# Strassen's algorithm for the gate and up products of two FFNs, and a down product in three chunks

## The chip, the cores and the metric

The kernel runs on one core of a Trainium2 chip. The metric is the device time of one execution in microseconds (us): 1136.71 us is the median of three runs before the change (1136.51 to 1138.03). The core has TensorE (PE) for matrix products, VectorE (DVE), ScalarE (ACT) and GpSimd (POOL) for elementwise work, and SyncE (SP), which issues the DMAs here. Each engine works through its own queue in order and waits on semaphores for the others. Products land in PSUM, and are read from there by VectorE and ScalarE.

## What is computed

The reference is one decoder layer over 512 tokens of width 1024, all in float32. Two of its sub-layers are the same gated FFN, one at the start and one at the end, with a hidden width of 2816; between them lie a token mixer and a cross-attention, which the change leaves alone.

```python
def rmsnorm(t, g):
    tf = t.astype(F32)
    y = tf * lax.rsqrt(jnp.mean(tf * tf, axis=-1, keepdims=True) + NORM_EPS)
    return (y * g.astype(F32)).astype(t.dtype)

def swiglu(h, w_gate, w_up, w_down):
    return (jax.nn.silu(h @ w_gate) * (h @ w_up)) @ w_down

h = rmsnorm(x, ffn1_norm[l])
x = x + 0.5 * swiglu(h, ffn1_w_gate[l], ffn1_w_up[l], ffn1_w_down[l])
...
h = rmsnorm(x, ffn2_norm[l])
x = x + 0.5 * swiglu(h, ffn2_w_gate[l], ffn2_w_up[l], ffn2_w_down[l])
return rmsnorm(x, final_norm)
```

## The kernel before

Activations are held transposed: X is eight tiles (`KD` = 8) of 128 channels by 512 tokens. Weights come tile by tile, so that one tile of a gate or up matrix is 128 outputs by 1024 inputs, as eight blocks of 128 x 128. The hidden width has 22 such tiles (`NF`), numbered f.

*Products in three parts.* To keep float32 precision, every operand is split in two (`split`, L102 to L105): ScalarE copies it to a rounded high part (L103), VectorE subtracts that to get the low part (L104). A product is then three matmuls (`mm3`, L124 to L129): high by high, high by low, low by high, accumulated in one PSUM bank. `load_weight` (L109) takes one of three raw buffers (tag `wraw`), loads it by a DMA on SP's queue, and splits it to one of three pairs `whi` and `wlo`.

*The norm is applied late.* `Norm.split` (L199) writes the high and low parts hH and hL of x times its gain; the factor of each token, R, is worked out beside the first matmuls (`factor`, L233: sums of squares that GpSimd adds up at L170, a column of them by TensorE, the inverse root by VectorE, and a broadcast by TensorE) and multiplied in when a product is read out of PSUM.

*The FFN* (`ffn`, L214). Two chunks of 11 hidden tiles (`NCHUNK`, `CF`). For each tile f the gate and the up product are run, each 8 x 3 matmuls of 512 columns into a bank of its own; `evacuate` (L241) multiplies both by R, applies SiLU, multiplies them and splits the result to hidH and hidL. After a chunk comes its part of the down product: for each of the eight output tiles d, 11 x 3 matmuls (`down_tile`, L219), after which VectorE adds half of it to X[d] (L230). In the second chunk of the first FFN, each finished X[d] goes to the next norm at once (`nxt.add`). In the last chunk of the last FFN the down product is run over the first and then the second half of the tokens, in matmuls of 256 columns, so that the final norm and the output of one half lie beside the products of the other; six of its eight weight tiles are kept for the second half (`weights`, L295), and the first two output tiles begin without the last hidden tile.

*Buffers and order.* PSUM has eight banks, four under `acc` and four under `aux`. The pool `hp` has 40 slots of 128 x 512 for split activations and a few others. The order of each engine's queue is made by a scheduler when the kernel is built: it goes by the order of the program where it can, and puts an instruction ahead of earlier ones that are not ready. GpSimd is used for sums of squares, a mask and a few memsets, and does nothing during gate, up and the first chunk of down, but for the memory rows.

Of the kernel before, what the change touches and what calls it, by code (L numbers as in the profile page):

```python
# [17 lines left out]
F32 = mybir.dt.float32  # L18
F32R = mybir.dt.float32r
# [5 lines left out]
P = 128  # L25
S = 512
# [1 line left out]
KD = D // P  # L28
FF = 2816
NF = FF // P  # L30
NCHUNK = 2
CF = NF // NCHUNK
NM = 256
NT = S // P
ATT_SCALE = 0.125
# [19 lines left out]
def body(tc, I, out):  # L55
# [3 lines left out]
    with ctx:  # L59
# [151 lines left out]
                self.square(d)  # L211


        def ffn(norm, gate, up, down, nxt, first=None, between=None):  # L214
            h = (norm.H, norm.L)
            with tc.tile_pool(name="ffn", bufs=2) as fp:
                R = None

                def down_tile(d, w, hid, tok, jj, acc=None, js=range(CF)):  # L219

                    if acc is None:
                        acc = acc_tile()[:, tok]
                    for (wH, wL), (j0, j1) in zip(w, jj):
                        for j in range(j0, j1):
                            if j in js:
                                mm3(acc, (wH, wL), hid, (slice(None), j - j0),
                                    (j, slice(None), tok), j == 0, j == CF - 1)
                    if CF - 1 not in js:
                        return acc
                    nc.vector.scalar_tensor_tensor(X[d][:, tok], acc, 0.5, X[d][:, tok],  # L230
                                                   op0=ALU.mult, op1=ALU.add)
# [6 lines left out]
                                norm.square(d)  # L238
                    return rows(norm.stats.column(D))

                def evacuate(ps, hid):  # L241
                    gp = fp.tile([P, S], F32, name="gp", tag="gp")
                    nc.vector.tensor_mul(gp, ps[0], R)  # L243
                    s = fp.tile([P, S], F32, name="s", tag="s")
                    nc.scalar.activation(s, gp, AF.Silu)
                    u = fp.tile([P, S], F32, name="u", tag="u")
                    nc.vector.tensor_mul(u, ps[1], R)  # L247
                    nc.vector.tensor_mul(u, s, u)
                    hH = fp.tile([P, S], F32R, name="hidH", tag="hidH", bufs=12)
                    hL = fp.tile([P, S], F32R, name="hidL", tag="hidL", bufs=12)  # L250
                    split(hH, hL, u)
                    hid[0].append(hH)
                    hid[1].append(hL)

                pending = []
                halves = ((0, 6), (6, CF))
                for c in range(NCHUNK):
                    hid = ([], [])
                    for j in range(CF):
                        f = c * CF + j  # L260
                        ps = []
                        for src in (gate, up):
                            if f == 0 and src is gate and first is not None:
                                w = first()
                            else:
                                w = load_weight(src[f], [KD, P])
                            acc = acc_tile()
                            for k in range(KD):
                                mm3(acc, w, h, (slice(None), k), k, k == 0, k == KD - 1)
                            ps.append(acc)  # L270
                            if first is not None and f == 1 and R is None:
                                R = factor()
                        pending.append(ps)
                        if first is not None and f == 0:
                            continue
                        if R is None:
                            R = factor()
                        while pending:
                            evacuate(pending.pop(0), hid)
                    if c < NCHUNK - 1 or nxt is not None:  # L280
                        for d in range(KD):
                            w = [load_weight(down[c, d, :, j0:j1, :], [j1 - j0, P])
                                 for j0, j1 in halves]
                            down_tile(d, w, hid, slice(0, S), halves)
                            if c == NCHUNK - 1:
                                nxt.add(d)
                            elif between is not None:
                                between(d)
                        continue


                    thirds = ((0, 4), (4, 8), (8, CF))
                    kept = {}

                    def weights(d, keep):  # L295
                        if d in kept:
                            return kept[d], thirds
                        if not keep:
                            return [load_weight(down[c, d, :, j0:j1, :], [j1 - j0, P])
                                    for j0, j1 in halves], halves  # L300
                        kept[d] = []
                        for j0, j1 in thirds:
                            raw = wp.tile([P, j1 - j0, P], F32, name="wraw3", tag="wraw")
                            nc.sync.dma_start(raw, down[c, d, :, j0:j1, :])
                            pair = tuple(h_tile("wk")[:, :(j1 - j0) * P]
                                         .rearrange("p (j m) -> p j m", m=P) for _ in range(2))
                            split(*pair, raw)
                            kept[d].append(pair)
                        return kept[d], thirds

                    for t0 in range(0, S, S // 2):
                        tok = slice(t0, t0 + S // 2)
                        stats = Stats(KD, S // 2, 1)
                        early = {}
                        if t0 == 0:
                            for d in range(2):
                                w, cut = weights(d, True)
                                early[d] = down_tile(d, w, hid, tok, cut, None, range(CF - 1))
                        for d in range(KD):
                            w, cut = weights(d, d < 6)  # L320
                            if d in early:
                                down_tile(d, w, hid, tok, cut, early[d], range(CF - 1, CF))
                            else:
                                down_tile(d, w, hid, tok, cut)
                            stats.add(X[d][:, tok])
                        R = rows(stats.column(D), 2, None)
                        for d in range(0, KD, 2):
                            o = fp.tile([P, 2, S // 2], F32, name="o", tag="o", bufs=4)
                            for e in range(2):
                                nc.vector.scalar_tensor_tensor(  # L330
                                    o[:, e], X[d + e][:, tok], gcol(G_FIN, d + e), R,
                                    op0=ALU.mult, op1=ALU.mult)
                            nc.sync.dma_start(out[d:d + 2, :, tok].rearrange("d p t -> p d t"), o)
# [495 lines left out]

def _down(w):  # L830

    return np.ascontiguousarray(w.reshape(NCHUNK, CF, P, KD, P).transpose(0, 3, 2, 1, 4))


def pack(x, mem, positions, ffn1_norm, ffn1_w_gate, ffn1_w_up, ffn1_w_down,
# [48 lines left out]
```

## Time and profile before

| | |
|---|---|
| median of 3 runs | 1136.71 us (1136.51 to 1138.03) |
| the profiled execution | 1139.12 us |
| its span, first to last instruction | 1137.3 us |
| mean granted TensorE clock | 0.993 of full speed |
| instructions | 13932, of which 5472 matmuls |
| moved by DMA | 110.79 MB, 97 GB/s over the span |

In the profile, L12 is line 12 of the kernel; PE and PEld are TensorE's matmuls and its weight loads, which overlap; a window or a row of the order of time starts with microseconds from the start of the span. A row of a group gives line, engine, operation, output and inputs, shapes and count, then busy time and mean length, then the idle time before it and what ended that. A row of the order of time gives its start, its length, engine, line, operation, tiles, and in brackets how long the engine had been idle and what released it. Matmuls are pipelined, so the length of one is more than the distance to the next, and the distance of starts says how fast they go.

### The profile page before, as it was taken

The numbers are of one execution on the slowest core, as the hardware profiler recorded it, in microseconds if no ns is written. First come the engines' busy times: TensorE is split into PE (matmuls) and PEld (weight loads), VectorE is DVE, ScalarE is ACT, GpSimd is POOL, SyncE is SP. The second block draws the span as 40 slices with busy tenths as digits, with TensorE's granted clock in tenths as the row PEclk, the third lists the DMA queues.
The fourth block names the chain that finished last, engine by engine and source line by source line (L and its number), as shares of the span: only waits on it lengthen the run. The fifth ranks groups of instructions, "written<-read, shape, count | busy, mean of one in ns | idle before, by whom it ended". The sixth has DMA issues, their size and how long they took to land. (4 is left out here: it accounts for less than half of the span.)

```text
span 1137.3 us, 13932 instructions
## 1 busy us (share of the span) xinstructions
PE 1121.1 (99%) x5472; PEld 936.4 (82%) x5472; DVE 589.2 (52%) x1023; ACT 422.6 (37%) x668; POOL 66.2 (6%) x82
## 2 busy tenths in 40 slices
PE   9999999999999999999999999999999999999996
PEld 7788888888888888877868988778888888888996
DVE  4544533444344456578797555455444334445542
ACT  6332322332233433567655344433222222233420
POOL 2000100000002000001121000120000000000011
PEclk9999999999999999999989999999999999999998
DMA  6322333222233423010135412132232333323511
GB/s 218 112 93 88 114 97 128 93 93 94 83 88 114 141 93 108 25 45 29 41 111 196 165 63 74 47 102 93 95 99 75 89 125 97 108 93 113 154 63 38
DMA packets 39698, 110.79 MB, mean 97 GB/s; under 512 B 4432, under 2 KB 9296, under 8 KB 39632
## 3 DMA queue, kind: packets, MB, share of 16 engines
q1 hardware_dynamic: 39632, 109.89, 30.1%
q8 instruction: 43, 0.70, 0.2%
q14 instruction: 23, 0.19, 0.1%
HBM read 107.78 MB, written 2.10 MB: 97 GB/s over the span
## 5 line engine op out<-in xcount | busy, mean ns | idle before, releaser
L103 ACT ACTIVATE whi<-wraw 128x1024 fp32r<-128x1024 f32 (+2 forms) x213 | 202.8, 953 | 522.0 <-PE acc L128 300.9
L104 DVE TENSOR_TENSOR wlo<-wraw,whi 128x1024 fp32r<-128x1024 f32 (+2 forms) x213 | 238.4, 1120 | 166.7 <-ACT whi L103 166.4
L127 PE MATMUL acc<-hH,whi 128*128 128x512 f32 x768 | 300.8, 392 | 0.6 <-ACT hH L202 0.6
L128 PE MATMUL acc<-hL,whi 128*128 128x512 f32 x768 | 299.3, 390 | 0.8 <-DVE hL L203 0.8
L129 PE MATMUL acc<-hH,wlo 128*128 128x512 f32 x768 | 299.3, 390 | 0.5 <-DVE wlo L104 0.5
L128 PEld LDWEIGHTS acc<-hL,whi 128*128 128x128 f32 x768 | 144.3, 188 | 31.6 <-DVE hL L203 1.5
L127 PEld LDWEIGHTS acc<-hH,whi 128*128 128x128 f32 x768 | 144.3, 188 | 31.6 <-ACT hH L202 1.0
L129 PEld LDWEIGHTS acc<-hH,wlo 128*128 128x128 f32 x768 | 144.2, 188 | 30.6 <-DVE wlo L104 1.0
L127 PE MATMUL acc<-hidH,whi 128*128 128x512 f32 (+1 forms) x308 | 115.5, 375 | 0.0
L129 PE MATMUL acc<-hidH,wlo 128*128 128x512 f32 (+1 forms) x308 | 115.3, 374 | 0.0
L128 PE MATMUL acc<-hidL,whi 128*128 128x512 f32 (+1 forms) x308 | 115.3, 374 | 0.0
L170 POOL TENSOR_TENSOR sq<-sq 128x512 f32<-128x512 f32 (+1 forms) x39 | 49.3, 1265 | 778.8 <-ACT sq L178 778.4
L247 DVE TENSOR_TENSOR u<-acc,R 128x512 f32<-128x512 f32 x44 | 30.4, 690 | 121.6 <-PE acc L129 121.6
L243 DVE TENSOR_TENSOR gp<-acc,R 128x512 f32<-128x512 f32 x44 | 30.4, 691 | 85.6 <-PE acc L129 81.7
L128 PEld LDWEIGHTS acc<-hidL,whi 128*128 128x128 f32 x308 | 58.0, 188 | 10.3
L127 PEld LDWEIGHTS acc<-hidH,whi 128*128 128x128 f32 x308 | 58.0, 188 | 10.2
L129 PEld LDWEIGHTS acc<-hidH,wlo 128*128 128x128 f32 x308 | 58.0, 188 | 10.2
L127 PE MATMUL acc<-whi,hH 128*128 128x512 f32 x160 | 62.6, 391 | 0.0
L129 PE MATMUL acc<-whi,hL 128*128 128x512 f32 x160 | 62.4, 390 | 0.0
L128 PE MATMUL acc<-wlo,hH 128*128 128x512 f32 x160 | 62.3, 389 | 0.0
L230 DVE SCALAR_TENSOR_TENSOR x<-acc,x 128x512 f32<-128x512 f32 (+1 forms) x40 | 23.3, 584 | 75.0 <-PE acc L129 75.0
L178 ACT ACTIVATE sq<-x 128x512 f32<-128x512 f32 (+1 forms) x48 | 26.0, 551 | 41.8 <-DVE x L230 39.2
(211 smaller groups left out, 1476.6 us busy)
## 6 DMA issues: line engine op xcount, KB each, us to landing
wraw<-up SPq DMA_DIRECT2D x44, 512.0 KB, 3.5
wraw<-gate SPq DMA_DIRECT2D x43, 512.0 KB, 3.4
wraw<-down SPq DMA_DIRECT2D x28, 384.0 KB, 3.1
wraw<-w_in SPq DMA_DIRECT2D x20, 512.0 KB, 3.5
wraw<-down SPq DMA_DIRECT2D x28, 320.0 KB, 2.8
wraw<-w_out SPq DMA_DIRECT2D x16, 256.0 KB, 2.6
wraw<-wv SPq DMA_DIRECT2D x8, 512.0 KB, 3.4
wraw<-wk SPq DMA_DIRECT2D x8, 512.0 KB, 4.0
```

The lines of the kernel that those rows point to most:

```text
L103: ins = nc.scalar.activation(hi, src, AF.Copy)
L104: nc.vector.tensor_sub(lo, src, f32(hi))
L127: nc.tensor.matmul(ps, lhsT=aH, rhs=bH, start=start, stop=False)
L128: nc.tensor.matmul(ps, lhsT=aH, rhs=bL, start=False, stop=False)
L129: nc.tensor.matmul(ps, lhsT=aL, rhs=bH, start=False, stop=stop)
L170: nc.gpsimd.tensor_add(self.parts[0], self.parts[0], sq)
L178: nc.scalar.activation(sq, src, AF.Square)
L230: nc.vector.scalar_tensor_tensor(X[d][:, tok], acc, 0.5, X[d][:, tok], op0=ALU.mult, op1=ALU.add)
L243: nc.vector.tensor_mul(gp, ps[0], R)
L247: nc.vector.tensor_mul(u, ps[1], R)
```

## The change

The gate and up products of the hidden tiles 2 to 21 are computed by a form of Strassen's algorithm with seven products instead of eight. The three halvings are: two weight tiles a1 and a2 (outputs), blocks 0 to 3 against 4 to 7 of the input channels, and tokens 0 to 255 (`LO`) against 256 to 511 (`HI`). Each of the seven products has 4 x 3 matmuls of 256 columns.

- `sums_of_h`, once for each FFN after hidden tile 0, builds sums and differences of the quarters of x times gain, and splits them (T13 and T24, 16 tiles of `hp`).
- `strassen_weights` loads two raw weight tiles, forms the sums of their halves (two on GpSimd, two on VectorE) and splits the seven left operands.
- `strassen` runs the products in the order 1, 2, 6, 5, 7, 3, 4. Products 1, 6, 7 and 4 accumulate in one `acc` bank, z; product 2 has an `aux` bank, 5 and 3 share another. ScalarE copies z after products 1 and 6, and the bank of product 5, to SBUF; VectorE adds up the four output quarters and multiplies them by R.
- Hidden tiles 0 and 1 stay plain products (`plain`, `evacuate`).
- The down product follows in three chunks of 8, 8 and 6 hidden tiles. In each, two output tiles start without the last pair of hidden tiles (three in the last chunk of the last FFN, where all eight weight tiles are now kept). The rotary tables and memory rows (`between`) move from the first chunk of the first FFN to its last.
- The FFN's pool is laid out anew, with working tiles shared under the tags `c` and `half`; the high parts of the hidden tiles move to `hp`.

```diff
-NCHUNK = 2
-CF = NF // NCHUNK
...
+        LO, HI = slice(0, S // 2), slice(S // 2, S)
+        KH = KD // 2
+        def sums_of_h(norm):
+            T13, T24 = ([], []), ([], [])
+            for k in range(KH):
+                xg = []
+                for d in (k, k + KH):
+                    t = hp.tile([P, S], F32, name="xg", tag="h")
+                    nc.vector.tensor_scalar_mul(t, X[d], gcol(norm.off, d))
+                    xg.append(t)
+                a, b = xg
+                t13 = hp.tile([P, S], F32, name="t13", tag="h")
+                nc.vector.tensor_sub(t13[:, LO], a[:, HI], a[:, LO])
+                nc.vector.tensor_sub(t13[:, HI], b[:, HI], a[:, HI])
+                t24 = hp.tile([P, S], F32, name="t24", tag="h")
+                nc.vector.tensor_sub(t24[:, LO], b[:, HI], t13[:, LO])
+                nc.vector.tensor_sub(t24[:, HI], b[:, LO], t24[:, LO])
+                for t, pair in ((t13, T13), (t24, T24)):
+                    pair[0].append(h_tile("tH"))
+                    pair[1].append(h_tile("tL"))
+                    split(pair[0][k], pair[1][k], t)
+            return T13, T24
...
-            with tc.tile_pool(name="ffn", bufs=2) as fp:
+            with tc.tile_pool(name="ffn", bufs=1) as fp:
...
+                def hidden(u, hid):
+                    hH, hL = h_tile("hidH"), fp.tile([P, S], F32R, name="hidL", tag="hidL", bufs=8)
+                def evacuate(ps, hid):
+                    gp = c_tile("gp")
+                    nc.vector.tensor_mul(gp, ps[0], R)
+                    nc.scalar.activation(gp, gp, AF.Silu)
+                    u = c_tile("u")
+                    nc.vector.tensor_mul(u, ps[1], R)
+                    nc.vector.tensor_mul(u, gp, u)
+                    hidden(u, hid)
...
+                def strassen_weights(src, j):
+                    a1 = wp.tile([P, KD, P], F32, name="wraw", tag="wraw")
+                    a2 = wp.tile([P, KD, P], F32, name="wraw2", tag="wraw")
+                    last["dma"] = nc.sync.dma_start(a1, src[2 * j])
+                    last["dma"] = nc.sync.dma_start(a2, src[2 * j + 1])
+                    k0, k1 = slice(0, KH), slice(KH, KD)
+                    s13 = fp.tile([P, 2, KH, P], F32, name="s13", tag="s13", bufs=2)
+                    nc.gpsimd.tensor_add(s13[:, 0], a2[:, k0], a2[:, k1])
+                    nc.gpsimd.tensor_sub(s13[:, 1], a1[:, k0], a2[:, k0])
+                    w1 = (wp.tile([P, KD, P], F32R, name="whi", tag="whi"),
+                          wp.tile([P, KD, P], F32R, name="wlo", tag="wlo"))
+                    split(w1[0], w1[1], a1)
+                    nc.vector.tensor_sub(a2[:, k0], s13[:, 0], a1[:, k0])
+                    w24 = tuple(fp.tile([P, 2, KH, P], F32R, name="w24" + n, tag="w24" + n, bufs=2)
+                                for n in "hl")
+                    split(w24[0][:, 0], w24[1][:, 0], a2[:, k0])
+                    w13 = tuple(fp.tile([P, 2, KH, P], F32R, name="w13" + n, tag="w13" + n)
+                                for n in "hl")
+                    split(w13[0], w13[1], s13)
+                    nc.vector.tensor_sub(a1[:, k0], a1[:, k1], a2[:, k0])
+                    split(w24[0][:, 1], w24[1][:, 1], a1[:, k0])
+                    w22 = tuple(fp.tile([P, KH, P], F32R, name="w22" + n, tag="w22" + n, bufs=2)
+                                for n in "hl")
+                    split(w22[0], w22[1], a2[:, k1])
+                    def of(w, i):
+                        return tuple(x[:, i] for x in w)
+                    return {1: of(w1, k0), 2: of(w1, k1), 6: of(w24, 0), 5: of(w13, 0),
+                            7: of(w13, 1), 3: of(w24, 1), 4: w22}
+                def strassen(src, j, T):
+                    w = strassen_weights(src, j)
+                    T13, T24 = T
+                    right = {1: (h, 0, LO), 2: (h, KH, LO), 3: (h, KH, HI), 4: (T24, 0, HI),
+                             5: (T13, 0, LO), 6: (T24, 0, LO), 7: (T13, 0, HI)}
+                    def product(ps, i, start):
+                        b, k0, tok = right[i]
+                        wH, wL = w[i]
+                        for k in range(KH):
+                            bH, bL = b[0][k0 + k][:, tok], b[1][k0 + k][:, tok]
+                            for n, (x, y) in enumerate(((wH, bH), (wH, bL), (wL, bH))):
+                                nc.tensor.matmul(ps, lhsT=x[:, k], rhs=y,
+                                                 start=start and k == 0 and n == 0,
+                                                 stop=k == KH - 1 and n == 2,
+                                                 skip_group_check=True)
+                    z = acc_tile()[:, HI]
+                    product(z, 1, True)
+                    p1 = half_tile("p1")
+                    nc.scalar.activation(p1, z, AF.Copy)
+                    b1 = aux_tile()[:, HI]
+                    product(b1, 2, True)
+                    c1, c2 = c_tile("c1"), c_tile("c2")
+                    nc.vector.tensor_add(c1[:, LO], b1, p1)
+                    product(z, 6, False)
+                    v = half_tile("v")
+                    nc.scalar.activation(v, z, AF.Copy)
+                    b5 = aux_tile()[:, HI]
+                    product(b5, 5, True)
+                    p5 = half_tile("p5")
+                    nc.scalar.activation(p5, b5, AF.Copy)
+                    product(z, 7, False)
+                    nc.vector.tensor_add(c2[:, HI], z, p5)
+                    product(b5, 3, False)
+                    nc.vector.tensor_add(c1[:, HI], b5, v)
+                    product(z, 4, False)
+                    nc.vector.tensor_mul(c2[:, LO], z, R[:, LO])
+                    nc.vector.tensor_mul(c1, c1, R)
+                    nc.vector.tensor_mul(c2[:, HI], c2[:, HI], R[:, HI])
+                    return c1, c2
+                T = None
+                chunks = ((0, 4), (4, 8), (8, NF // 2))
+                for c, (j0, j1) in enumerate(chunks):
+                    for j in range(j0, j1):
+                        if j == 0:
+                            pending = []
+                            for f in (0, 1):
+                                ps = [plain(f, gate)]
+                                if f == 1 and R is None:
+                                    R = factor()
+                                ps.append(plain(f, up))
+                                pending.append(ps)
+                                if first is None and f == 0:
+                                    R = factor()
+                                if R is not None:
+                                    while pending:
+                                        evacuate(pending.pop(0), hid)
+                                if f == 0:
+                                    T = sums_of_h(norm)
+                            continue
+                        g = strassen(gate, j, T)
+                        for t in g:
+                            nc.scalar.activation(t, t, AF.Silu)
+                        u = strassen(up, j, T)
+                        for a, b in zip(g, u):
+                            nc.vector.tensor_mul(b, a, b)
+                            hidden(b, hid)
+                    f0, n = 2 * j0, 2 * (j1 - j0)
+                    if c < len(chunks) - 1 or nxt is not None:
+                        early = {}
+                        for d in range(2):
+                            w = [load_weight(down[d, :, f0:f0 + n, :], [n, P])]
+                            early[d] = w, down_tile(d, w, hid, slice(0, S), None, range(n - 2))
+                        for d in range(KD):
+                            if d in early:
+                                w, acc = early[d]
+                                down_tile(d, w, hid, slice(0, S), acc, range(n - 2, n))
...
+                    cut = ((0, 4), (4, 6))
...
+                            for d in range(3):
+                                early[d] = down_tile(d, weights(d), hid, tok, None, range(n - 2),
+                                                     cut)
...
-    return np.ascontiguousarray(w.reshape(NCHUNK, CF, P, KD, P).transpose(0, 3, 2, 1, 4))
+    return np.ascontiguousarray(w.reshape(NF, P, KD, P).transpose(2, 1, 0, 3))
```

108 lines of the change are left out of this document (38 added, 70 removed).

## The prediction

> **What bounds the kernel now.** I read the page first: busy shares, then the chain that ended last; after that the windows of the stages, the order of time, and the groups by line and shape.
>
> ```profile
> PE 1121.1 (99%) x5472; PEld 936.4 (82%) x5472; DVE 589.2 (52%) x1023; ACT 422.6 (37%) x668; POOL 66.2 (6%) x82
> ...
> PE 32%; DVE 0%; issue 0%; ACT 0%; DVEq 0%; ACTq 0%
> 131.00:219.00 88.00, 88.00 (x392) 72.92 (x391) 35.60 (x53) 21.77 (x27) 0.00 (x0) 1.00 0.32 100
> 13.30:34.30 21.00, 20.47 (x95) 15.87 (x93) 10.16 (x22) 10.04 (x15) 7.77 (x6) 1.00 0.49 162
> 763.80:782.80 19.00, 18.98 (x84) 15.20 (x85) 9.36 (x23) 6.85 (x8) 0.00 (x0) 1.00 0.32 103
> ```
>
> TensorE is busy nearly all the span, the chain of waits names hardly anything else, and in the first down product (131 to 219 us) VectorE works 35.6 of 88 us and ScalarE 21.8 (columns of a window: its length, then PE, PEld, DVE, ACT, POOL busy). The granted clock is 1.00. So the kernel is bound by how many matmuls TensorE streams, and busy time misleads there, since neighbours overlap. The pitch has to come from starts:
>
> ```profile
> 1029.66 0.39 PE L127 MATMUL acc<-hH,whi 128*128 128x512 f32 x1
> ...
> 1046.89 0.39 PE L128 MATMUL acc<-hL,whi 128*128 128x512 f32 x1
> ...
> 1060.26 0.28 PE L127 MATMUL acc<-hidH,wk 128*128 128x256 f32 x1
> ...
> 1076.93 0.28 PE L128 MATMUL acc<-hidL,wk 128*128 128x256 f32 x1
> ```
>
> Between the first two lie 76 steps, 17.23/76 = 0.2267 us for 512 columns; between the last two 139 steps, 16.67/139 = 0.120 us for 256 columns. Half the columns cost 53%, not 50%. The profiled execution took 1139.12 us (span 1137.3), the median is 1136.71. I add differences to the median.
>
> **The change, part by part.**
>
> *Matmuls of gate and up.* Two output tiles of one weight matrix now take 2 x 8 x 3 = 48 matmuls of 512 columns, 48 x 0.2267 = 10.88 us. A Strassen call has 7 products of 4 x 3 matmuls of 256 columns, 84 x 0.120 = 10.08 us. That is 0.80 us less, not the eighth that 7 for 8 suggests. Tiles 0 and 1 stay plain, so there are 10 pairs x 2 matrices x 2 FFNs = 40 calls: **-32.0 us** of matmul.
>
> *Down in chunks of 8, 8 and 6.* The number of matmuls is the same. In the last FFN the half-token part shrinks from 11 tiles to 6: 2 x 8 x 5 x 3 = 240 matmuls of 0.120 become 120 of 0.2267, 28.8 against 27.2: **-1.6 us**. Eight more residual updates per FFN (L230, about 0.69 us each) lie beside down products in which VectorE is 60% idle. A third handover from hidden tiles to down is added per FFN; two d tiles started early without the last pair give 2 x 6 x 3 x 0.2267 = 8.2 us of cover, against about 5 us to finish a pair (working below). I cost it at nothing; without that cover it would be 5 us each, 10 in all. The rotary tables and memory rows move to the last chunk: a few us of ACT and DVE under 4 us of PE per tile, nothing.
>
> *What a call costs the other engines.*
>
> ```profile
> L104 DVE TENSOR_TENSOR wlo<-wraw,whi 128x1024 fp32r<-128x1024 f32 x139 | 173.2, 1246 | 100.9 <-ACT whi L103 100.7
> L103 ACT ACTIVATE whi<-wraw 128x1024 fp32r<-128x1024 f32 x139 | 147.2, 1060 | 376.9 <-PE acc L128 184.9 <-issue 150.2 <-PE acc L129 40.3
> L103 ACT ACTIVATE hidH<-u 128x512 fp32r<-128x512 f32 x44 | 27.8, 633 | 35.2 <-DVE u L248 35.2
> L103 ACT ACTIVATE kH<-acc 128x256 fp32r<-128x256 f32 x8 | 2.9, 365 | 0.0
> L230 DVE SCALAR_TENSOR_TENSOR x<-acc,x 128x256 f32<-128x256 f32 x16 | 6.7, 424 | 30.1 <-PE acc L129 30.1
> L509 DVE TENSOR_SCALAR s<-s,rz 128x512 f32<-128x512 f32 x8 | 3.9, 481 | 0.0
> 34.24 0.68 DVE L247 TENSOR_TENSOR u<-acc,R 128x512 f32<-128x512 f32 x1
> 34.84 0.68 DVE L243 TENSOR_TENSOR gp<-acc,R 128x512 f32<-128x512 f32 x1
> 699.20 1.23 DVE L104 TENSOR_TENSOR wlo<-wraw,whi 128x1024 fp32r<-128x1024 f32 x1 [3.23 <-ACT whi L103]
> 700.34 0.68 DVE L104 TENSOR_TENSOR qL<-acc,qH 128x512 fp32r<-128x512 f32 x1
> ```
>
> Back to back, VectorE takes 0.60 us for 512 elements and 1.14 for 1024, so about 0.33 for 256. Per call: weights 2 x 1.14 + 5 x 0.60 = 5.3; collecting the products 5 x 0.33 + 0.60 = 2.3; the hidden tiles of a pair (two products, two low parts, 2.4) shared by two calls 1.2. Together **8.8 us of VectorE per 10.08 us of PE**. ScalarE: 2 x 1.06 + 3 x 0.63 + 3 x 0.37 + 1.25 = 6.4 us. GpSimd, idle here until now, gets two sums of 512 per call, and these are not free for VectorE:
>
> ```profile
> 737.04 0.75 DVE L203 SCALAR_TENSOR_TENSOR hL<-x,gains,hH 128x512 fp32r<-128x512 f32 x1
> ...
> 738.30 1.72 DVE L104 TENSOR_TENSOR wlo<-wraw,whi 128x1024 fp32r<-128x1024 f32 x1
> 739.95 1.77 DVE L203 SCALAR_TENSOR_TENSOR hL<-x,gains,hH 128x512 fp32r<-128x512 f32 x1
> 737.14 1.80 POOL L170 TENSOR_TENSOR sq<-sq 128x512 f32<-128x512 f32 x1 [2.88 <-ACT sq L178]
> 739.81 1.36 POOL L170 TENSOR_TENSOR sq<-sq 128x512 f32<-128x512 f32 x1 [0.87 <-ACT sq L178]
> 584.83 0.68 DVE L619 TENSOR_TENSOR yo<-acc,R 128x512 f32<-128x512 f32 x1
> 584.62 1.41 POOL L170 TENSOR_TENSOR sq<-sq 128x512 f32<-128x512 f32 x1 [0.27 <-ACT sq L178]
> ```
>
> Beside a GpSimd sum the same low part took 1.77 instead of 0.75 us, and a weight's 1.72 instead of 1.23: 1.0 and 0.5 lost, a mean of 0.75. The op at 584.83, which reads PSUM and one SBUF tile, lost nothing. The Trainium skill, "SBUF — State Buffer", section "Who interferes with whom", says that a VectorE instruction with two SBUF inputs and a GpSimd instruction that reads SBUF exclude each other, the later one blocking fully. These rows agree, and by that rule a sum could cost VectorE its whole length; it is rival A that carries this.
>
> Two sums at 0 to 1.36 us each cost VectorE 0 to 2.7 us per call; I take 1.5, from the two rows, so 10.3 us per call. That exceeds 10.08, but calls aren't all alike. Before chunks 1 and 2 stands a down product of 8 x 24 x 0.2267 = 43.5 us with about 8 x (1.14 + 0.60) = 14 us of VectorE in it, so the weights of the first call and a half, about 10 us, can be ready. Chunk 1 then needs 8 x 10.3 - 10 = 72 of 80.6 us. Chunk 0 (6 calls) has no such lead: 62 for 60.5 us. What stays is jitter: z, one PSUM bank, passes 1, 6, 7, 4, and PE may go on only when it has been read. Each handover is covered by one product, 12 x 0.120 = 1.44 us. The read of z after product 7 is VectorE's (0.42 us); behind a blocked op of 1.72 that has just begun, PE waits 0.7 us. Such ops fill about a third of a call, so about 0.15 us on the mean; ScalarE's three reads (0.37 behind at most 1.06) just fit. With chunk 0's deficit and misplaced queue orders I take 0.3 us per call, bounds 0 and 1.4 (VectorE at 8.8 + 2.7): **+12 us** (0 to 57). DMA bytes of gate and up are unchanged; down has fewer transfers.
>
> *The sums of h.* At each FFN's start VectorE gets 8 scalings (481 ns, 0.40 back to back), 16 halves at 0.33 and 8 low parts at 0.60: 13.3 us; ScalarE 8 x 0.63 = 5. They run beside tiles 0 and 1.
>
> ```profile
> 16.33 8.17 POOL L170 TENSOR_TENSOR sq<-sq 128x512 f32<-128x512 f32 x6 [15.89 <-ACT sq L178]
> 34.38 0.51 PE L127 MATMUL acc<-hH,whi 128*128 128x512 f32 x1
> 763.81 0.50 PE L128 MATMUL acc<-hL,whi 128*128 128x512 f32 x1 [0.48 <-DVE hL L203]
> 778.60 1.22 DVE L104 TENSOR_TENSOR wlo<-wraw,whi 128x1024 fp32r<-128x1024 f32 x1
> ```
>
> FFN2: from the last hL (763.8) to the end of tile 1 (about 782.8) VectorE works 9.4 us, 1.2 of it for a tile 2 that is gone, so 10.8 are free. Needed before product 6, which first reads the sums, are 13.3 + w1 1.14 + w24 1.2 + lock 1.5 = 17.1, less 2.9 for products 1 and 2: about 4 us late. FFN1: from 13.3 to 34.3 us VectorE works 10.2 us, 2.5 for tile 2, so 13.3 are free; needed are 17.1 + 6 x 0.75 for the squares that GpSimd adds there, less 2.9: about 6 us late. **+10 us**, bounds 4 (gaps used better) and 25 (all behind PE).
>
> *Sum:* -32.0 - 1.6 + 10 + 12 = -11.6, so 1136.7 - 11.6 = **1125 us**.
>
> **The rivals.**
>
> A, *VectorE becomes the bound through the GpSimd sums* (slower). For it: 8.8 us of work, of which only five small ops read PSUM, and the 1.0 us in the 739.95 row. Against: idle VectorE in down. An in-order VectorE that is late with z holds PE, so the lead is worth less than I count. At 11.0 us per call (8.8 + 2 x 1.1) the 12 become 37: 1150 us. It decides from 10.67 us per call, (33.6 - 10)/40 = 0.59 over the matmuls.
>
> B, *three raw buffers feed two raw tiles per call* (slower). The next a2 can only load when a1 is done with.
>
> ```profile
> wraw<-up SPq DMA_DIRECT2D x44, 512.0 KB, 3.5
> ```
>
> Then 3.5 for the DMA, 2 x 1.36 to 1.8 for the sums, and about 4.3 for the differences and their parts follow: 10.5 to 11.4 us a call. Against: two buffers of each derived tile and the lead absorb most within 8 calls. At 10.9 the 12 become 33: 1146 us.
>
> C, *all is hidden*: starts cost 4, calls 0.1 each: 1136.7 - 33.6 + 8 = 1111 us.
>
> D, *a draw*: stalls eat the 33.6 us nearly exactly, 1134 to 1139.
>
> **How the numbers follow.** Forecast 0.36, C 0.17, D 0.12, A 0.23, B 0.12. Faster by over 0.2% (what a measurement can tell from no change): 0.53; within it 0.12; slower 0.35. The range reaches from C's better half, 1107, to A with 11.2 us per call, 1160; about 2 in 10 lie outside. Where the time is shorter, 1112 to 1134 is the forecast's own range.
>
> **What would show it.** Matmuls of 256 columns at 0.120 us in the calls, calls of 10.2 to 10.6 us; DVE near 90% in Strassen stretches; low parts of 1.7 us beside POOL; PE idle at product 6 of each FFN's first call, 4 to 6 us in sum. A call length over 10.7 us with PE released by DVE would prove A, with ACT or POOL waiting for wraw B. A pitch over 0.126 would undo the first term.

## The result, and the profile after

The changed kernel takes 1207.22 us (median of 4 runs, 1204.36 to 1210.1) against 1136.97 us before: 1.062 times the time, 95% interval 1.058 to 1.065. It was forecast at 1125 us, with a range from 1107 to 1160. The profiled execution has a span of 1208.1 us, 70.8 more than before.

The page of the changed kernel, busy times and the chain that ended last:

```profile
PE 1121.5 (93%) x6792; PEld 991.7 (82%) x6792; DVE 805.9 (67%) x1445; ACT 529.2 (44%) x906; POOL 182.9 (15%) x162
...
PE 45%; DVE 12%; POOL 4%; DMA 4%; ACT 2%; issue 2%; DVEq 0%; POOLq 0%; ACTq 0%; SPq 0%
```

Before, the chain held little but TensorE. Now VectorE, GpSimd and DMAs stand in it with a fifth of the span: something makes TensorE wait. The windows of the first FFN's three Strassen stretches (6, 8 and 6 calls):

```profile
47.80:118.70 70.90, 65.58 (x507) 62.94 (x506) 55.66 (x89) 34.40 (x60) 13.62 (x10) 0.96 0.31 98
162.10:257.30 95.20, 84.53 (x674) 82.69 (x673) 68.93 (x112) 43.31 (x74) 16.47 (x13) 0.98 0.30 95
300.70:372.10 71.40, 63.86 (x506) 62.58 (x505) 51.71 (x93) 32.12 (x57) 10.86 (x9) 0.98 0.31 100
```

A call takes 70.9/6, 95.2/8 and 71.4/6 = 11.8 to 11.9 us, where its matmuls need 10.08; yet VectorE, the third figure after the length, is busy 72 to 79%, not 90%. So a bound of plain VectorE work isn't what one sees. Counted from the first start of a stretch to the start that follows its last matmul, these are 70.8, 95.1 and 71.2 us, and those of the second FFN 76.9, 94.6 and 72.4. Added up by such starts, the difference to before is:

| stretch | forecast, us | measured, us |
|---|---|---|
| fewer and shorter matmuls | -33.6 | -33.6 |
| 40 calls over 10.08 us each (480.8 - 403.2) | +12 | +77.6 |
| first call of FFN1 at 47.8, tile 2 before at 34.4 | +6 | +13.4 |
| second FFN, first matmul to first call, 26.3 against 24.6 | +4 | +1.7 |
| last down product of FFN1, 39.5 against 144 x 0.2267 = 32.6 | 0 | +6.9 |
| end of the last call to the end of the span, 54.1; before 77.1, less 240 x 0.120 | 0 | +5.8 |

That makes 71.8 us. The other -1.0 is lost by the kernel before: its first down product (132.5 to 193.3 us) takes 60.8 us, where 264 matmuls need 59.8.

Inside a call, one can see it happen. The order of time of the changed kernel, first TensorE, then ScalarE, VectorE and GpSimd at the same place:

```profile
212.34 0.28 PE L345 MATMUL aux<-hH,wlo 128*128 128x256 f32 x1
...
212.69 0.28 PE L345 MATMUL aux<-hH,wlo 128*128 128x256 f32 x1
...
213.06 0.28 PE L345 MATMUL aux<-hH,wlo 128*128 128x256 f32 x1
214.82 0.38 PE L345 MATMUL acc<-tH,w24h 128*128 128x256 f32 x1 [1.49 <-ACT p L353]
...
217.67 0.28 PE L345 MATMUL aux<-tH,w13l 128*128 128x256 f32 x1
218.88 0.39 PE L345 MATMUL acc<-tH,w13h 128*128 128x256 f32 x1 [0.94 <-ACT v L360]
```
```profile
212.40 0.63 ACT L101 ACTIVATE w24h<-wraw 128x512 fp32r<-128x512 f32 x1 [3.77 <-DVE wraw L313]
212.94 1.04 ACT L101 ACTIVATE whi<-wraw 128x1024 fp32r<-128x1024 f32 x1
213.89 0.61 ACT L101 ACTIVATE w22h<-wraw 128x512 fp32r<-128x512 f32 x1
214.41 0.36 ACT L353 ACTIVATE p<-acc 128x256 f32<-128x256 f32 x1
```
```profile
207.69 0.42 DVE L366 TENSOR_TENSOR c<-acc,p 128x256 f32<-128x256 f32 x1 [0.39 <-PE acc L345]
211.62 0.69 DVE L313 TENSOR_TENSOR wraw<-s,wraw 128x512 f32<-128x512 f32 x1 [3.52 <-POOL s L308]
```
```profile
209.05 1.28 POOL L307 TENSOR_TENSOR s<-wraw 128x512 f32<-128x512 f32 x1 [6.36 <-DMA wraw<-up]
210.30 1.29 POOL L308 TENSOR_TENSOR s<-wraw,wraw 128x512 f32<-128x512 f32 x1
```

Read from below: GpSimd gets a2 at 209.05 and has both sums at 211.6. VectorE has stood 3.5 us with the difference (L313) at the head of its queue. ScalarE has stood 3.8 us behind it, and then splits three weights of a later call before it copies z (214.41). TensorE waits for that copy 1.5 us, and at 218.88 for the next one. All its waits for these two copies add up to 34.9 us. All 40 differences together kept VectorE idle 95.3 us:

```profile
L308 POOL TENSOR_TENSOR s<-wraw,wraw 128x512 f32<-128x512 f32 x40 | 60.0, 1499 | 0.0
L307 POOL TENSOR_TENSOR s<-wraw 128x512 f32<-128x512 f32 x40 | 56.6, 1415 | 536.3 <-DMA wraw<-gate 292.6 <-DMA wraw<-up 182.5 <-DVE c L368 26.8
...
L313 DVE TENSOR_TENSOR wraw<-s,wraw 128x512 f32<-128x512 f32 x40 | 27.7, 691 | 95.3 <-POOL s L308 95.3
L102 DVE TENSOR_TENSOR w24l<-wraw,w24h 128x512 fp32r<-128x512 f32 x80 | 54.3, 684 | 4.1 <-ACT w24h L101 3.7
```

(groups by line and shape of the changed kernel). The last row matters too: the low parts w24l keep their 684 ns, so the sums do not lengthen them here. The first reading was therefore rival B: a2 comes late because three raw buffers feed two tiles a call. GpSimd's 475.1 us of waiting for wraw (second row) is also the sign that the prediction had named for B.

Part of the loss is a slower clock. In eleven pieces of 3.4 to 10.2 us, 58 us together, the granted clock is half, and matmuls of 256 columns then start 0.213 us apart instead of 0.120. The kernel before has one such piece of 6.8 us (both have one more at the end of the span, not counted here). One of the eleven, as a window and in the order of time:

```profile
172.30:175.40 3.10, 3.10 (x16) 3.10 (x16) 2.13 (x4) 0.95 (x1) 0.00 (x0) 0.50 0.00 0
```
```profile
172.66 0.41 PE L345 MATMUL acc<-tL,w13h 128*128 128x256 f32 x1
...
175.22 0.41 PE L345 MATMUL aux<-hL,w24h 128*128 128x256 f32 x1
```

Summed over the matmuls in these pieces that is about 17 us against 3 before, some 10 of them in the calls. This is worked out from the starts; no run here tests it apart from the waits.

### The profile page after: what moved, and what is told of

It reads as the page before. It is cut to its first block, busy times and chain, and to the rows that moved or that the text cites. A ratio compares the mean times of both kernels' runs of the same rounds, so it can differ in the third digit from the quotient of the medians.

```text
span 1208.1 us, 17314 instructions
## 1 busy us (share of the span) xinstructions
PE 1121.5 (93%) x6792; PEld 991.7 (82%) x6792; DVE 805.9 (67%) x1445; ACT 529.2 (44%) x906; POOL 182.9 (15%) x162
## 4 chain that ended last, share of the span: by engine, by line
PE 45%; DVE 12%; POOL 4%; DMA 4%; ACT 2%; issue 2%; DVEq 0%; POOLq 0%; ACTq 0%; SPq 0%
PE acc L127 10%; PE acc L125 10%; PE acc L126 10%; PE acc L345 5%; PE aux L345 3%; DMA wraw<-up 2%; PE aux L125 2%; POOL s L308 2%; POOL s L307 2%; PE aux L127 2%; PE aux L126 2%; DMA wraw<-gate 2%; DVE wlo L102 1%; DVE w13l L102 1%; DVE w24l L102 1%
## 5 line engine op out<-in xcount | busy, mean ns | idle before, releaser
L102 DVE TENSOR_TENSOR wlo<-wraw,whi 128x1024 fp32r<-128x1024 f32 (+2 forms) x157 | 187.2, 1194 | 86.6 <-ACT whi L101 86.4
L307 POOL TENSOR_TENSOR s<-wraw 128x512 f32<-128x512 f32 x40 | 56.6, 1415 | 536.3 <-DMA wraw<-gate 292.6
L125 PE MATMUL acc<-hidH,whi 128*128 128x512 f32 x304 | 119.3, 392 | 0.0
L127 PE MATMUL acc<-hidH,wlo 128*128 128x512 f32 x304 | 119.0, 392 | 0.0
L126 PE MATMUL acc<-hidL,whi 128*128 128x512 f32 x304 | 118.9, 391 | 0.0
L313 DVE TENSOR_TENSOR wraw<-s,wraw 128x512 f32<-128x512 f32 x40 | 27.7, 691 | 95.3 <-POOL s L308 95.3
L101 ACT ACTIVATE w24h<-wraw 128x512 fp32r<-128x512 f32 x80 | 49.6, 626 | 76.3 <-DVE wraw L313 44.5
L126 PEld LDWEIGHTS acc<-hidL,whi 128*128 128x128 f32 x304 | 57.5, 189 | 11.8
L125 PEld LDWEIGHTS acc<-hidH,whi 128*128 128x128 f32 x304 | 57.5, 189 | 11.8
L345 PE MATMUL acc<-tH,w13h 128*128 128x256 f32 x160 | 48.6, 304 | 19.5 <-ACT v L360 19.5
L308 POOL TENSOR_TENSOR s<-wraw,wraw 128x512 f32<-128x512 f32 x40 | 60.0, 1499 | 0.0
L102 DVE TENSOR_TENSOR w24l<-wraw,w24h 128x512 fp32r<-128x512 f32 x80 | 54.3, 684 | 4.1 <-ACT w24h L101 3.7
L127 PE MATMUL acc<-hH,wlo 128*128 128x512 f32 x128 | 50.9, 398 | 3.8 <-DVE wlo L102 3.8
```

What stands on the lines that cost most here:

```text
L101: ins = nc.scalar.activation(hi, src, AF.Copy)
L102: nc.vector.tensor_sub(lo, src, f32(hi))
L125: nc.tensor.matmul(ps, lhsT=aH, rhs=bH, start=start, stop=False)
L126: nc.tensor.matmul(ps, lhsT=aH, rhs=bL, start=False, stop=False)
L127: nc.tensor.matmul(ps, lhsT=aL, rhs=bH, start=False, stop=stop)
L307: nc.gpsimd.tensor_add(s13[:, 0], a2[:, k0], a2[:, k1])
```

## The experiments

Each time here, but for the versions at the end, is the median of two executions, which lie up to 4 us apart.

**A fourth raw buffer.** If B holds, this frees the way.

```diff
-                    return fp.tile([P, S], F32, name=name, tag="c", bufs=5)
+                    return fp.tile([P, S], F32, name=name, tag="c", bufs=4)
...
-                    return fp.tile([P, S // 2], F32, name=name, tag="half", bufs=5)
+                    return fp.tile([P, S // 2], F32, name=name, tag="half", bufs=3)
...
-                    a2 = wp.tile([P, KD, P], F32, name="wraw2", tag="wraw")
+                    odd.append(j)
+                    pool, tag = (wp, "wraw") if len(odd) % 2 else (fp, "raw4")
+                    a2 = pool.tile([P, KD, P], F32, name="wraw2", tag=tag)
```

> A fourth raw buffer in the FFN's pool (every second a2), paid for with the small buffers (p1, v, p5: 3 instead of 5; c: 4 instead of 5). Theory B (the way of a2 from the release of a1's buffer through DMA, GpSimd sums and VectorE differences sets the length of a call, and ScalarE and VectorE stand in their queues behind it while PE waits for the copies of z): a call falls from 11.85 to 10.3 to 10.8 us, 40 x 1.0 to 1.5 = 40 to 60 us less, 1147 to 1167 us; GpSimd's wait for the DMA of a2 is no longer what VectorE waits on. Theory A (VectorE with the lock of the GpSimd sums is the bound): nothing changes, 1200 to 1210 us.

**Its control**, the smaller buffers alone (the first two edits, and the tag `c` of the last tile `o` with them).

> The control for the fourth raw buffer: the small buffers cut in the same way (p1, v, p5: 3 instead of 5; c: 4 instead of 5), with three raw buffers. Both theories: 1205 to 1212 us, as the changed kernel. If it is slower by more than 5 us, the small buffers matter and the comparison goes to this run.

Measured: 1216.74 us with the fourth buffer, 1205.52 us for the control. B's gain of 40 to 60 us isn't there; the time is even above A's bracket. The same two groups with the fourth buffer:

```profile
L102 DVE TENSOR_TENSOR w24l<-wraw,w24h 128x512 fp32r<-128x512 f32 x80 | 81.7, 1026 | 5.9 <-ACT w24h L101 5.6
...
L317 DVE TENSOR_TENSOR wraw<-s,wraw 128x512 f32<-128x512 f32 x40 | 33.7, 843 | 22.2 <-POOL s L312 22.2
```

The wait for the sums fell from 95.3 to 22.2 us, as B says it should, but now w24l takes 1026 ns instead of 684. By the order of time, about 96 of the sums' 126 us now lie beside VectorE operations with two inputs in SBUF, against 35 of 117 in the changed kernel, and VectorE's busy time rises from 805.9 to 847.9 us. The sums came earlier, ran beside VectorE's work, and lengthened it: what had been a wait became a lock.

**The sums on VectorE**, with three raw buffers and with four.

```diff
-                    nc.gpsimd.tensor_add(s13[:, 0], a2[:, k0], a2[:, k1])
-                    nc.gpsimd.tensor_sub(s13[:, 1], a1[:, k0], a2[:, k0])
+                    nc.vector.tensor_add(s13[:, 0], a2[:, k0], a2[:, k1])
+                    nc.vector.tensor_sub(s13[:, 1], a1[:, k0], a2[:, k0])
```

> The two sums of raw halves on VectorE instead of GpSimd, three raw buffers. Theory B: the way is shorter by 3.0 - 1.2 = 1.8 us a call, but VectorE has 8.8 + 1.2 = 10.0 us of work per call: calls of 10.6 to 11.2 us, 1157 to 1180 us. Theory A (lock): the lock is gone, VectorE at 10.0 us is just under the matmuls: 10.2 to 10.6 us a call, 1140 to 1157 us. If VectorE's plain work were the bound it would get slower, by up to 40 x 1.2 = 48 us.

> Both edits: a fourth raw buffer and the sums on VectorE. Theory B: with the way no longer the bound, the sums on VectorE only cost work; as the fourth buffer alone or up to 15 us slower, 1147 to 1180 us. Theory A: as the sums on VectorE alone, 1140 to 1157 us.

Measured: 1156.54 and 1153.26 us. More work on VectorE made the kernel 50.7 us faster, and calls in the second stretch last 84.1/8 = 10.5 us. The first time lies at the border between the brackets of A and B. Now the fourth buffer gives 3 us. These two times don't separate A from B (1153.26 lies in both brackets); it is the fourth buffer with the sums still on GpSimd that speaks against B.

Two explanations were left. Q: the order of the queues, with the copies of z behind VectorE's wait. L: the lock itself.

**The order bound.** Everything of a call's weights but the split of a1 and the GpSimd sums is queued behind the call before's copies.

```diff
+                    with ExitStack() as order:
+                        for key in ("p5", "c2"):
+                            if key in last:
+                                order.enter_context(tc.issue_after(last[key].ins))
+                        nc.vector.tensor_sub(a2[:, k0], s13[:, 0], a1[:, k0])
...
+                    last["p5"] = nc.scalar.activation(p5, b5, AF.Copy)
...
+                    last["c2"] = nc.vector.tensor_add(c2[:, HI], z, p5)
```

> The changed kernel with its GpSimd sums and three raw buffers; only the order is bound: of a call's weights, all that comes after the split of a1 stands in ScalarE's queue behind the call before's copy of product 5 and in VectorE's queue behind its read of z after product 7. Theory Q (the GpSimd sums cost because VectorE's differences, and ScalarE's splits after them, wait for the sums at the head of their queues, with the copies of z behind them): the copies no longer stand behind, calls fall from 11.85 to 10.3 to 10.9 us, 1145 to 1170 us. Theory L (the sums cost because they lock VectorE's second operand out): the same locks, 1195 to 1210 us.

Measured: 1206.35 us, nothing gained. The waits of VectorE with this order:

```profile
DVE c L370 <- PE acc L349: 75.7, 25, 4.0
...
DVE wraw L317 <- POOL s L308: 30.7, 26, 2.4
```

VectorE waits less for the sums (30.7 us), but now at the read of z (L370) for TensorE, and the weights behind that come late. This order brought a wait of its own, so alone it speaks weakly against Q.

**The lock by itself.** To the kernel with its sums on VectorE, two GpSimd sums per call are added for which nobody waits (the tag `half` gets 3 buffers, to make room).

```diff
+                    junk = fp.tile([P, KH, P], F32, name="junk", tag="junk")
+                    nc.gpsimd.tensor_add(junk, f32(w22[0]), f32(w22[1]))
+                    nc.gpsimd.tensor_sub(junk, f32(w22[0]), f32(w22[1]))
```

> The sums on VectorE as in the earlier run at 1156.5 us, and on GpSimd two sums of 512 per call of tiles that lie there anyway, into a tile that nobody reads (work added, nobody waits for it). Theory L: the locks are back, 80 x 0.6 to 1.0 us of VectorE, which has little left: 1190 to 1210 us. Theory Q: nobody waits for the sums, only the lock is paid: 1157 to 1180 us.

**Its control**: nearly as much GpSimd time that reads nothing (the tags `half` and `c` cut to 3 and 4; the first memset and the tiles aren't shown).

```diff
+                    nc.vector.tensor_copy(tiny, junk[:, 0:1])
+                    for _ in range(3):
+                        nc.gpsimd.memset(junk, 0.0)
```

> The control for the idle GpSimd sums (1212.9 us): the sums on VectorE, and per call three memsets of 1024 on GpSimd, about as long as two sums, into a tile of which VectorE copies one column per call (40 copies, about 5 us of VectorE; the small buffers cut as in the runs with four raw buffers). They write and read nothing. If two operands of VectorE and what GpSimd reads exclude each other, VectorE's ops keep their lengths: 1153 to 1165 us. If any GpSimd work beside it, or the notes between the engines, slowed VectorE: 1180 to 1215 us.

Measured: 1212.92 us with the idle sums, 1162.18 us with the memsets, against 1156.54 us without either. No wait of any engine ends at an idle sum. In the order of time of that kernel, VectorE and then GpSimd:

```profile
205.39 2.31 DVE L102 TENSOR_TENSOR wlo<-wraw,whi 128x1024 fp32r<-128x1024 f32 x1
207.62 0.41 DVE L360 TENSOR_TENSOR c<-aux,p 128x256 f32<-128x256 f32 x1
207.95 1.45 DVE L102 TENSOR_TENSOR w24l<-wraw,w24h 128x512 fp32r<-128x512 f32 x1
...
210.70 0.69 DVE L102 TENSOR_TENSOR w24l<-wraw,w24h 128x512 fp32r<-128x512 f32 x1 [0.70 <-ACT w24h L101]
```
```profile
205.00 1.60 POOL L326 TENSOR_TENSOR junk<-w22h,w22l 128x512 f32<-128x512 f32 x1 [4.29 <-DVE w22l L102]
206.69 2.16 POOL L327 TENSOR_TENSOR junk<-w22h,w22l 128x512 f32<-128x512 f32 x1
```

The low part that meets a sum at 207.95 takes 1.45 us, the one at 210.70, with no sum beside it, 0.69. The addition at 207.62, which reads PSUM and one SBUF tile, keeps its 0.41 us inside the sum. Over the whole run the 31 w24l that lay beside a sum took 1495 ns on the mean, the other 49 took 683. Groups of the kernel with idle sums:

```profile
L327 POOL TENSOR_TENSOR junk<-w22h,w22l 128x512 f32<-128x512 f32 x40 | 69.6, 1740 | 3.1
...
L102 DVE TENSOR_TENSOR w24l<-wraw,w24h 128x512 fp32r<-128x512 f32 x80 | 79.4, 998 | 6.2 <-ACT w24h L101 5.9
L102 DVE TENSOR_TENSOR w13l<-s,w13h 128x1024 fp32r<-128x1024 f32 x40 | 59.9, 1496 | 0.3
```

and of the one with memsets:

```profile
L332 POOL MEMSET junk<- 128x1024 f32 x120 | 114.9, 958 | 153.4 <-DVE tiny L330 148.9
...
L102 DVE TENSOR_TENSOR w24l<-wraw,w24h 128x512 fp32r<-128x512 f32 x80 | 54.3, 684 | 8.4 <-ACT w24h L101 8.2
L102 DVE TENSOR_TENSOR w13l<-s,w13h 128x1024 fp32r<-128x1024 f32 x40 | 48.8, 1220 | 0.7 <-ACT w13h L101 0.2
```

135 us of sums take w24l from 684 to 998 ns and cost 56 us. The memsets are a weaker control than was meant. Nothing of a call holds them back, so they were put ahead: all 120 lie in the first 145 us and between 733 and 887 us, and none beside the calls in four of the six Strassen stretches. So the 1162.18 us doesn't show what memsets beside every call would cost. What is shown is single operations: 18 low parts of 128x1024 that met a memset took 1222 ns, and 105 that met no GpSimd work 1221. An operation with one input did grow: the four parts of dg take 1.64 us beside memsets, and 0.87 us in the kernel with its sums on VectorE and nothing added (second line):

```profile
791.57 1.64 DVE L149 TENSOR_SCALAR dg<-const,rcoly 128x128 f32<-128x128 f32 x4
788.01 0.87 DVE L149 TENSOR_SCALAR dg<-const,rcoly 128x128 f32<-128x128 f32 x4
```

The page of the kernel with its sums on VectorE has VectorE busy for 836.3 us, that with the idle sums:

```profile
PE 1118.8 (93%) x6792; PEld 988.5 (82%) x6792; DVE 900.6 (74%) x1525; ACT 531.0 (44%) x906; POOL 203.0 (17%) x162
```

64 us more for 80 sums, 0.80 us each. So the lock is shown: GpSimd sums that nobody waits for cost 56 us, about as much as the changed kernel loses by its own (50.7). How much of that loss in the changed kernel is lock and how much is waiting isn't shown by this. The Trainium skill, "SBUF — State Buffer", section "Who interferes with whom", says that a VectorE instruction with two SBUF inputs doesn't contend with a GpSimd instruction that only writes. The 18 low parts that met a memset (1222 ns against 1221) agree.

**The starts.** First the sums of h left out (products 4 to 7 take h in their place, so part of the computation is missing), then, in the first FFN, moved behind the norm's factor.

```diff
         def sums_of_h(norm):
+            if True:
+                return ((norm.H, norm.L),) * 2
```

> The changed kernel without the sums and differences of x times gain at each FFN's start: the products 4 to 7 take h in place of T13 and T24, so that part of the computation is left out. If the starts cost what a comparison of the two traces says (13 us in the first FFN, where the root of the norm stands in VectorE's queue between the sums, and 3 us and a slow first chunk, 6 us, in the second), it falls by 16 to 24 us to 1183 to 1192 us; by the 10 us of the prediction, to 1197 us.

```diff
-                                if f == 0:
+                                if f == (1 if first is not None else 0):
                                     T = sums_of_h(norm)
```

> The changed kernel with one line moved: in the first FFN the sums of h stand behind tile 1 and the norm's factor in the order of the program, not ahead of tile 1. If PE stands still at tile 2 of the first FFN because the small operations of the norm's root lie in VectorE's queue between the sums of h, the root ends early again, the hold of about 9 us before the first call shrinks to 4 or less, and the first calls take part of it back since the sums come later: 1199 to 1206 us. If the work of the sums itself is what holds PE there, wherever it stands: 1205 to 1210 us.

Measured: 1189.71 us without the sums, 17.5 less; and 1214.18 us with the sums moved, above both brackets. In the latter the norm's root does end early, and the first call starts at 41.0 instead of 47.8 us, but the first six calls last 86.2 instead of 70.8 us. The sums of h have no cover at either place; the root between them was only where it showed.

**Versions that draw level with the kernel before, and beat it.** They stand on the kernel with its sums on VectorE and a fourth raw buffer (1153.26 us), and each adds to the one ahead of it. More plain tiles give the sums of h cover: four, with the sums behind the factor (an edit not shown here); then the rotary tables and memory rows back in the first down product; then six plain tiles.

```diff
-                        if j == 0:
-                            pending = []
-                            for f in (0, 1):
+                        if j < 2:
+                            if j == 0:
+                                pending = []
+                            for f in (2 * j, 2 * j + 1):
```

> The sums on VectorE, the fourth raw buffer, and two things more: four instead of two hidden tiles are plain (36 calls instead of 40), and the sums of h come behind the norm's factor in the order of the program. Costs 4 x 0.8 = 3.2 us of matmul; the sums of h get 22 us more of cover. From 1153 us: -16 to -22 for the starts, + 3: 1134 to 1142 us. If the starts are not what remains, 1150 to 1156 us.

```diff
-                                if f == 1:
+                                if f == (1 if first is not None else 0):
                                     T = sums_of_h(norm)
...
-                                if between is not None:
-                                    between(d)
+                            elif c == 0 and between is not None:
+                                between(d, c_tile)
...
-                    raw = hp.tile([P, S], F32, name="mraw0", tag="h")
+                    raw = tile("mraw0")
```

> As the run at 1136.0 us (sums on VectorE, fourth raw buffer, four plain tiles), with two things more: in the second FFN the sums of h come right behind the norm's factor (one tile earlier), and the rotary tables and memory rows go back to the first chunk's down product, in tiles of the tag c. The last down product of the first FFN should lose the 5 to 7 us that it has over 144 x 0.2267, the second FFN's first calls up to 4 us: 1125 to 1133 us. If those stretches are slow for other reasons: 1133 to 1138 us.

```diff
-                        if j < 2:
+                        if j < 3:
```

> As the run before it, with six plain hidden tiles (32 calls instead of 40, 3.2 us of matmul more than with four). If the first calls of an FFN still run behind the sums of h (11.1 to 11.6 us instead of 10.3), 4 calls x 1 us x 2 = up to 8 us go with them: 1122 to 1132 us; else 3 us slower than the run before it.

| kernel | us | to before, 95% interval |
|---|---|---|
| four plain tiles | 1135.97 | 0.999 (0.998 to 1.000) |
| and the rows moved back | 1124.12 | 0.989 (0.987 to 0.990) |
| and six plain tiles | 1119.25 | 0.983 (0.982 to 0.985) |

The first can't be told from the kernel before. The other two gain 1.1% and 1.7%, a little more than was expected of them.

The second stretch of the last one, by windows:

```profile
142.80:224.10 81.30, 81.30 (x674) 80.94 (x673) 71.62 (x119) 43.64 (x72) 0.00 (x0) 1.00 0.34 109
```

81.3/8 = 10.16 us a call with VectorE 88% busy, its sums included, and TensorE without a pause: 0.08 over the matmuls. The granted clock is half for 10.2 us of this run, against 41.0 us with the sums on VectorE alone.

## Why the prediction was wrong

**The matmuls: right.** 256 columns go at 0.120 us in the calls too (212.34 to 213.06 in six steps), and 10.16 us a call shows that 0.72 of the 0.80 us can be had. The bound it gave for its first term is off: the pitch that undoes it is 10.88/84 = 0.1295 us, not 0.126. That the clock could fall to half was not in it.

**The cost of a call: the step that failed.** The prediction put a GpSimd sum at "1.5, from the two rows" per call, let a lead from the down products pay for it, and kept 0.3 us a call as jitter, +12 us. Measured are 1.9 us a call, +77.6 us, above even its bound of 57. Two things were wrong in it. The lead did nothing: in the first FFN the stretches behind a down product (11.9 us a call) are no faster than the first (11.8). And the price of a sum was counted as lengthening alone; in the changed kernel it comes mostly as VectorE's wait for the sums, 95.3 us, and where that wait is taken away it comes as a lock. VectorE's own 8.8 us and two sums of 1.42 and 1.50 us, one after the other, make 11.7, close to the 11.8 to 11.9 measured with three buffers, and to the 93.5/8 = 11.7 of the second stretch with four. That they take turns in the changed kernel is worked out from this, and it isn't the whole account: with four buffers VectorE is busy for only 74.9 of those 93.5 us, and the clock is half for 10.2 of them. That the sums on GpSimd cost 50.7 us is shown, and that the lock costs 0.80 us a sum is shown by the idle sums; how wait, queue order and clock share the rest stays open.

**The rivals.** A, the bound through the GpSimd sums, was nearest, given 0.23 and 1150 us: right in place, too small in size, since it counted 2 x 1.1 us and no copies of z behind. Operations that grow by the lock, as A has it, are seen with the fourth buffer and with the idle sums; in the changed kernel the sums cost mostly as a wait. VectorE was full in neither: with the idle sums it is busy for 86.1 of 96.2 us in the second stretch, 89%, and the fastest version bears 88% without a pause of TensorE. B saw the late a2 that the trace shows, and the prediction's own sign, POOL waiting for wraw, spoke for B; but with the fourth buffer VectorE's wait for the sums fell to 22.2 us without a gain, while POOL, which has nothing else to do, still waited 285.8 us for the gate weights. The 0.3 us of jitter that the forecast kept hold in the second stretch once GpSimd is out of it: 10.5 - 10.08 = 0.4 us with the sums on VectorE. Over all 40 calls of that kernel it is 0.8 us, most of it in the first stretch of each FFN (10.8 and 12.4 us a call), where the sums of h lie.

**The starts: right in kind, too small.** Forecast 10 us (its own figures give 3.4 and 5.4, rounded up to 4 and 6); without the sums of h the kernel is 17.5 us faster. The order of time shows one thing the prediction passed over, the small operations of the root strung between sums of h on VectorE:

```profile
38.17 0.42 DVE L232 TENSOR_TENSOR t<-xg,t 128x256 f32<-128x256 f32 x1
38.51 0.16 DVE L139 TENSOR_TENSOR rcolt<-rcoly 128x4 f32<-128x4 f32 x1
38.58 0.69 DVE L102 TENSOR_TENSOR w24l<-wraw,w24h 128x512 fp32r<-128x512 f32 x1
...
45.79 0.87 DVE L149 TENSOR_SCALAR dg<-const,rcoly 128x128 f32<-128x128 f32 x4
```

In the first FFN TensorE stood about 8 us for dg. Beside the squares that GpSimd adds up there, halves took 1.51 us instead of 0.42 (one at 23.75 us, L230), the same lock.

**The handovers: wrong.** Costed at nothing, they show 6.9 and 5.8 us. In the first FFN the memory rows that were moved there put 5 us of GpSimd sums beside VectorE. Moving them back came with a gain of 11.9 us, together with the earlier sums of h; the share of each wasn't measured apart. In the last FFN TensorE goes from the last call (1153.85) to the down product (1156.90) with a wait of 2.8 us for the split of a down weight.

## What to carry to other kernels

Work put on an idle engine isn't free when its operations and those of the nearly full engine exclude each other: before a sum goes to GpSimd, price what it takes from VectorE's operations with two inputs (0.80 us a sum here), and ask who stands behind its result in an in-order queue. A saving on the bound engine counts only while every other engine stays below it with room for its waits; a lead in buffers doesn't help an engine that meets the wait at the head of its queue. And a fixed cost at a stage's start is hidden by giving it cover: two more pairs of plain tiles cost 6.4 us of matmul in both FFNs together, and the kernel with them was the fastest. A control has to be looked up in the trace before it is believed: the memsets did not run where the sums did.

## What had not been expected of the hardware

Sums on GpSimd that nothing waits for cost VectorE 0.80 us each and the kernel 56 us, and they grow themselves, from 1.28 us alone to 1.63 and 1.74 us on the mean. GpSimd memsets left VectorE's operations with two inputs at their length (1222 ns against 1221), but not the scalings by one column (dg, 1.64 us instead of 0.87). In pieces of 3.4 to 10.2 us TensorE's granted clock fell to half, 58 us of the changed kernel against 6.8 before. Pauses alone don't decide it: the second stretch with idle sums takes 96.2 us, with TensorE busy for 84.5 of them, at a clock of 1.00.
